# First layer's attention: three engines in program order, the modulation in single steps between key blocks

## The chip, the cores and the metric

The kernel runs on one core of a Trainium2 chip. The metric is device time in microseconds (us), the median of several runs. The engines are TensorE (PE in the profile, its weight loads PEld), VectorE (DVE), ScalarE (ACT), GpSimd (POOL) and SyncE (SP), which issues nearly all DMAs.

## The reference

Two layers; each is attention, then a gated MLP with a causal convolution, with RMSNorms and a modulation by a conditioning vector `c`. The first layer's attention is "stick-breaking" (16 heads of 64, 512 positions, width 1024):

```python
mod = jnp.einsum('bd,dm->bm', silu(c), w_mod[i]) + b_mod[i]
sh_a, sc_a, gt_a, sh_f, sc_f, gt_f = jnp.split(mod, 6, axis=-1)
h = modulate(rmsnorm(x, g_mix_pre[i]), sh_a, sc_a)
q, k, v = (split_heads(t) for t in jnp.split(jnp.einsum('bsd,de->bse', h, w_qkv[i]), 3, axis=-1))
# stick-breaking, for each block of queries:
log_beta = log_sigmoid(z); log_1mb = where(strict, log_sigmoid(-z), 0)
after = cumsum(log_1mb, reverse=True) - log_1mb
a = where(strict, exp(log_beta + after), 0)          # times v
o = merge_heads(a @ v) @ w_o[i]
x = x + gt_a * rmsnorm(o, g_mix_post[i])             # then the MLP, with sh_f, sc_f, gt_f
```

## The kernel before

All matrix products are made of three fp32r matmuls: each operand is split in a high part (a cast on ACT, L192) and a low part (a subtraction, L193), by DVE or, for most weights of the attention, by GpSimd (`wh`, `wl`; for late tiles of `w_o` `sh`, `sl`).

`attention` runs over heads. In the pass for head h, for each of four query blocks `qb` from 3 down to 0 (512, 384, 256, 128 keys wide), `scores` writes a PSUM bank `ps` (L380); `stick` makes two sigmoids on ACT (`bt`, `ps`: L389, L390), a running product on DVE (a scan, L391, into `om` for the two wide blocks, else in place) and a product `bt` (L392; on GpSimd for the two wide blocks, else on DVE). Between the blocks the head before (`late`) goes on: `transposed` turns its probabilities on PE (`pa`, L414) and splits them (`ah` on ACT, `al` on DVE). After the fourth block `weighted` multiplies them with the values into `po` (L429 with `ah`, L430 with `al`); the result goes through ACT and DVE (`of`, L434 and L435), and after an odd head it is split (`oh`, `ol`). Between all of this `fill` puts pieces of other PE work, `UNITS` many a head (some ten): projections of later heads (`proj`, bank `pqk`, 8 pieces each; then `queries` makes `qa`, `qb` or `keys` makes `kh`, `kl`, by turns on ACT and DVE from that one bank), values (`pv`, `v`) and the start of the output projection (`project`).

`mod_part` computes one sixth of the modulation in steps: it sums eight tiles of `w_mod` (512 KB each, DMA into `wm`, three buffers shared with `ah`, `al` and `gp` of this part) times an element of `csil` on DVE (`acc`, 128x1024, L143; the first of some parts L141), splits the sum (L146, L148), sums over partitions with matmuls `pm` (L160, L161), and makes a row (`gt`, L163) or columns (eight diagonals, L128). In the first layer `Background` does three parts (`GT_A`, `SC_F`, `SH_F`) behind the attention's heads: three steps at the end of each pass for a head, from head 2 on, at a lower priority.

`Stream` loads weight tiles (`raw`: DMA into `wf`, three buffers) two tiles ahead of use and splits them at once.

What sets the order: PE and SP run in the order in which the program is written, in the whole kernel. In `begin`, ahead of the first attention, ACT, DVE and GpSimd do as well; elsewhere a scheduler orders these three by priorities (the place in the program) and its own idea of when things are ready.

Of the kernel before, what the change touches and what calls it, by code (L numbers as in the profile page):

```python
# [37 lines left out]
def trunk(ctx, tc, x, c, w_mod, b_mod, g_mix_pre, g_mix_post, w_qkv, w_o, w_fg, b_fg,  # L38
# [8 lines left out]
    def nm(s):  # L47
        serial[0] += 1
        return f"{s}_{serial[0]}"
# [10 lines left out]
    def t4(s, dt=F32):  # L60
        return sb.tile([P, D], dt, tag="t4", name=nm(s), bufs=3)
# [65 lines left out]

        nc.vector.tensor_tensor_reduce(junk(P), src, idn, 1.0, 0.0, op0=ALU.mult, op1=ALU.add, accum_out=dst)  # L128

    def mod_part(l, comp):  # L130
        row = comp in (GT_A, GT_F)
        acc = sb.tile([P, D], F32, tag="acc", name=nm("acc"), bufs=1)
        lo_c = comp * D
        if row:
            nc.gpsimd.memset(acc, 0.0)
            nc.sync.dma_start(acc[0:1, :], b_mod[l : l + 1, lo_c : lo_c + D])
        for d in range(ND):
            w = t4("wm")
            nc.sync.dma_start(w, w_mod[l, d * P : (d + 1) * P, lo_c : lo_c + D])
            if d == 0 and not row:  # L140
                nc.vector.tensor_scalar(acc, w, csil[:, 0:1], None, op0=ALU.mult)  # L141
            else:
                nc.vector.scalar_tensor_tensor(acc, w, csil[:, d : d + 1], acc, op0=ALU.mult, op1=ALU.add)  # L143
            yield
# [27 lines left out]
        made[l, comp] = res  # L172

    class Background:
        def __init__(self, parts):
            self.gens = [mod_part(*p) for p in parts]

        def step(self, n=1):
            while n and self.gens:
# [15 lines left out]
    def raw(src, inner):  # L195
        w = sb.tile([P, 1024], F32, tag="wf", name=nm("wf"), bufs=3)
        v = w.rearrange("p (a b) -> p a b", b=inner)
        nc.sync.dma_start(v, src)
        return w

    def w_tile(src, inner, engine=None):
        w = raw(src, inner)
        hi = sb.tile([P, 1024], F32R, tag="wh", name=nm("wh"), bufs=3)
        lo = sb.tile([P, 1024], F32R, tag="wl", name=nm("wl"), bufs=3)
        split(hi, lo, w, engine)
        return hi, lo

    def w_slots(src, inner, engine=None):
        w = raw(src, inner)
        res = []  # L210
# [4 lines left out]
        return res  # L215

    class Stream:
        def __init__(self):
            self.keys, self.fns, self.got, self.at = [], [], {}, 0

        def add(self, key, fn):
            self.keys.append(key)
            self.fns.append(fn)

        def upto(self, i):
            while self.at <= min(i, len(self.keys) - 1):
                self.got[self.keys[self.at]] = self.fns[self.at]()
                self.at += 1

        def need(self, key, ahead=2):  # L230
            i = self.keys.index(key)
            self.upto(i + ahead)
            return self.got[key]

    ws = Stream()
# [283 lines left out]
    def attention(l, qk, vt, ot, filler, units, bg):  # L519
# [4 lines left out]
        for h in range(NH + 1):  # L524
# [17 lines left out]
            for qb in range(NT - 1, -1, -1):  # L542
                if h < NH:
                    ps, n = scores(l, hd, qb, qk[p, 0], qk[p, 1])
                    probs[qb] = stick(ps, n) if l % 2 == 0 else fox(ps, qb, cums[h])
                    fill()
                if turned:
                    at = next(turned)
                    fill()
            fill(2)  # L550
            if late:
                drain(turned)
# [2 lines left out]
                        fill()  # L555
            fill(12)
            late = (probs, h)
            with tc.high_priority(offset=-100):
                bg.step(3 if h > 1 else 0)


    def begin(vt, qk):
# [196 lines left out]

    cums_of = {}  # L760
    for l in range(DEPTH):
        bg = Background([(l, GT_A), (l, SC_F), (l, SH_F)] if l == 0 else [])
        scale = -0.125 if l % 2 else 0.125
        vt, qk = {}, {}
        if l == 0:
# [172 lines left out]
```

## Time and profile before

| | before |
|---|---|
| median of 3 runs | 1312.1 us (1309.64 to 1312.73) |
| profiled execution | 1313.45 us, span 1311.7 us |
| mean granted clock of TensorE | 0.99 |
| PE, DVE, ACT, POOL busy, share of the span | 95%, 63%, 47%, 22% |
| first layer's attention, first score matmul of head 0 to that of head 14 | 74.17 to 253.62 us |

A row of a timeline has start (us), duration (us), engine, line, operation, output and inputs (buffer numbers left out), shape, count, and in brackets the idle time just before with what ended it. A row of the waits has who waited for whom, us in total, times, and the longest. Durations of neighbours on one engine overlap by some hundredths.

### The profile page before, as it was taken

Reading aid. Unit: us, or ns where it says so; the run is one execution under the profiler, and the core shown is the slowest. Engines: PE = TensorE matmul, PEld = TensorE weight load, DVE = VectorE, ACT = ScalarE, POOL = GpSimd, SP = SyncE. Lnnn points to the kernel's source line nnn. Section 1 sums busy time; section 2 is a strip of 40 time slices with the busy share of each in tenths; the row PEclk is TensorE's granted clock in tenths of the full one; section 3 lists DMA queues with packets and bytes.
Section 4 is the critical chain, followed back from the end, with each engine's and each line's share of the span. In section 5 each row is a group of like instructions: output and inputs, shape, how many; then the busy total and the mean of one; then the engine's idle time right before and its main releaser. Section 6 shows DMA issues by size and latency. Waiting matters only on the chain.

```text
span 1311.7 us, 17096 instructions
## 1 busy us (share of the span) xinstructions
PE 1252.5 (95%) x6244; PEld 1050.0 (80%) x6244; DVE 829.0 (63%) x1455; ACT 617.3 (47%) x1182; POOL 293.7 (22%) x326
## 2 busy tenths in 40 slices
PE   5898978999999999999999999999999999999997
PEld 4676867789887788888888789887898888888886
DVE  7978889756868887532344777786775444443233
ACT  5466645757434333321356556666753333332121
POOL 3586544631000000000022744554100000000000
PEclk8999988999999999999999999999999999999999
DMA  8652533221667766332411533332254333333331
GB/s 273 197 177 97 162 113 128 81 85 45 225 209 245 235 219 217 111 96 97 144 35 43 169 113 104 106 114 80 80 190 131 97 96 96 97 97 97 96 96 64
DMA packets 174857, 169.19 MB, mean 129 GB/s; under 512 B 6937, under 2 KB 151729, under 8 KB 174773
## 3 DMA queue, kind: packets, MB, share of 16 engines
q1 hardware_dynamic: 174596, 168.04, 41.0%
q8 instruction: 49, 0.80, 0.2%
q14 instruction: 36, 0.29, 0.1%
q10 hardware_dynamic: 176, 0.07, 0.0%
HBM read 165.92 MB, written 2.16 MB: 128 GB/s over the span
## 4 chain that ended last, share of the span: by engine, by line
PE 64%; DVE 9%; ACT 5%; DMA 3%; issue 2%; POOL 1%; POOLq 0%; DVEq 0%; SPq 0%; ACTq 0%
PE pgu L267 11%; PE pgu L268 11%; PE pgu L266 11%; PE pd L267 6%; PE pd L268 6%; PE pd L266 6%; PE pqk L266 2%; PE pqk L267 2%; PE pqk L268 1%; PE ps L380 1%; DMA wf<-in_w_ffn_gate_dram 1%; DVE fx L404 1%; PE pa L414 1%; ACT junk L287 1%; PE po L430 1%
## 5 line engine op out<-in xcount | busy, mean ns | idle before, releaser
L192 ACT CAST wh<-wf 128x1024 fp32r<-128x1024 f32 (+2 forms) x178 | 185.3, 1041 | 317.2 <-PE pgu L267 151.1
L193 DVE TENSOR_TENSOR wl<-wf,wh 128x1024 fp32r<-128x1024 f32 x122 | 149.2, 1223 | 217.9 <-ACT wh L192 215.6
L267 PE MATMUL pgu<-htl,wh 128*128 128x512 f32 (+1 forms) x736 | 276.9, 376 | 0.5 <-DVE htl L328 0.5
L266 PE MATMUL pgu<-hth,wh 128*128 128x512 f32 (+1 forms) x736 | 276.9, 376 | 0.0
L268 PE MATMUL pgu<-hth,wl 128*128 128x512 f32 (+1 forms) x736 | 276.9, 376 | 0.0
L193 POOL TENSOR_TENSOR wl<-wf,wh 128x1024 fp32r<-128x1024 f32 (+3 forms) x56 | 132.8, 2376 | 230.4 <-ACT wh L192 218.6
L267 PEld LDWEIGHTS pgu<-htl,wh 128*128 128x128 f32 x736 | 138.9, 189 | 26.1 <-DVE htl L328 0.9
L266 PEld LDWEIGHTS pgu<-hth,wh 128*128 128x128 f32 x736 | 139.0, 189 | 25.0
L268 PEld LDWEIGHTS pgu<-hth,wl 128*128 128x128 f32 x736 | 138.8, 189 | 25.2
L279 POOL TENSOR_TENSOR r<-v,mhalf 128x1 f32<-128x1 f32 x32 | 17.8, 557 | 450.7 <-DVE v L275 450.7
L266 PE MATMUL pd<-wh,yh 128*128 128x512 f32 x288 | 112.0, 389 | 0.0
L267 PE MATMUL pd<-wl,yh 128*128 128x512 f32 x288 | 112.0, 389 | 0.0
L268 PE MATMUL pd<-wh,yl 128*128 128x512 f32 x288 | 112.0, 389 | 0.0
L143 DVE SCALAR_TENSOR_TENSOR acc<-wm,csil,acc 128x1024 f32<-128x1024 f32 x74 | 101.1, 1366 | 15.2 <-DMA wm<-in_w_mod_dram 14.6
L266 PE MATMUL pqk<-hth,wh 128*128 128x512 f32 (+1 forms) x240 | 100.9, 420 | 0.0
L268 PE MATMUL pqk<-hth,wl 128*128 128x512 f32 (+1 forms) x240 | 93.9, 391 | 0.5 <-POOL wl L193 0.5
L267 PE MATMUL pqk<-htl,wh 128*128 128x512 f32 (+1 forms) x240 | 93.6, 390 | 0.0
L850 ACT ACTIVATE cv<-cv 128x512 f32<-128x512 f32 x44 | 27.8, 632 | 102.7 <-DVE cv L849 98.0
L266 PE MATMUL pv<-wh,hth 128*128 128x256 f32 (+1 forms) x224 | 69.9, 312 | 0.1
L268 PE MATMUL pv<-wh,htl 128*128 128x256 f32 (+1 forms) x224 | 67.1, 299 | 1.1 <-DVE htl L664 1.0
L267 PE MATMUL pv<-wl,hth 128*128 128x256 f32 (+1 forms) x224 | 66.9, 299 | 0.0
L851 DVE TENSOR_TENSOR cv<-cv,pgu 128x512 f32<-128x512 f32 x44 | 30.2, 686 | 52.9 <-PE pgu L268 46.9
(194 smaller groups left out, 2513.4 us busy)
## 6 DMA issues: line engine op xcount, KB each, us to landing
wm<-in_w_mod_dram SPq DMA_DIRECT2D x80, 512.0 KB, 4.9
wf<-in_w_ffn_gate_dram SPq DMA_DIRECT2D x44, 512.0 KB, 4.4
wf<-in_w_ffn_up_dram SPq DMA_DIRECT2D x44, 512.0 KB, 3.7
wf<-in_w_ffn_down_dram SPq DMA_DIRECT2D x44, 512.0 KB, 3.5
wf<-in_w_qkv_dram SPq DMA_DIRECT2D x41, 512.0 KB, 3.8
wm<-in_w_mod_dram SPq DMA_DIRECT2D x32, 256.0 KB, 4.2
wf<-in_w_o_dram SPq DMA_DIRECT2D x16, 512.0 KB, 3.6
cum<-cumd SPq DMA_DIRECT2D x16, 512.0 KB, 4.1
```

The costliest lines, as they stand in the source:

```text
L143: nc.vector.scalar_tensor_tensor(acc, w, csil[:, d : d + 1], acc, op0=ALU.mult, op1=ALU.add)
L192: nc.scalar.copy(hi, src)
L193: (engine or nc.vector).tensor_tensor(lo, src, hi.bitcast(F32), op=ALU.subtract)
L266: nc.tensor.matmul(ps, ah, bh, start=first, stop=False)
L267: nc.tensor.matmul(ps, ah, bl, start=False, stop=False)
L268: nc.tensor.matmul(ps, al, bh, start=False, stop=last)
L279: nc.gpsimd.tensor_tensor(r, v, mhalf, op=ALU.pow)
L287: nc.scalar.activation(junk(), src, AF.Square, scale=1.0 / 32.0, accum_out=m)
L380: nc.tensor.matmul(ps[:, :n], q[hd][:, qs], k[hd][i][:, :n], start=i == 0, stop=i == 1)
L404: nc.vector.tensor_scalar(t[:, :n], t[:, :n], r, None, op0=ALU.mult)
L850: nc.scalar.activation(a, a, AF.Silu)
L851: nc.vector.tensor_tensor(a, a, u, op=ALU.mult)
```

## The change

In the first layer's attention ACT, DVE and GpSimd now also run in program order. The modulation takes one step behind each of the query blocks 3, 2 and 1 of the heads from 2 on, not three at the end of a pass; each `wm` load is written one step ahead of its use, and a part has twelve steps (the first only loads). A weight tile's DMA is still written two tiles ahead, but its split now comes with the next tile's load (`lag`). Elsewhere `lag` and `ahead` are 0.

```diff
-    def mod_part(l, comp):
+    def mod_part(l, comp, ahead=0):
...
+        tiles = []
+
+        def load(d):
+            tiles.append(t4("wm"))
+            nc.sync.dma_start(tiles[d], w_mod[l, d * P : (d + 1) * P, lo_c : lo_c + D])
+
+        load(0)
+        if ahead:
+            yield
         for d in range(ND):
-            w = t4("wm")
-            nc.sync.dma_start(w, w_mod[l, d * P : (d + 1) * P, lo_c : lo_c + D])
+            if d + ahead < ND and d + ahead:
+                load(d + ahead)
+            w = tiles[d]
...
     def w_tile(src, inner, engine=None):
         w = raw(src, inner)
+        yield
...
         def upto(self, i):
-            while self.at <= min(i, len(self.keys) - 1):
-                self.got[self.keys[self.at]] = self.fns[self.at]()
+            while len(self.loaded) <= min(i, len(self.keys) - 1):
+                self.loaded.append(self.fns[len(self.loaded)]())
+                next(self.loaded[-1])
+                self.parts(len(self.loaded) - 1 - self.lag)
+
+        def parts(self, i):
+            while self.at <= i:
+                self.got[self.keys[self.at]] = next(self.loaded[self.at])
                 self.at += 1
 
         def need(self, key, ahead=2):
             i = self.keys.index(key)
             self.upto(i + ahead)
+            self.parts(i)
             return self.got[key]
...
                 if turned:
                     at = next(turned)
                     fill()
+                if qb and h > 1:
+                    bg.step()
...
             late = (probs, h)
-            with tc.high_priority(offset=-100):
-                bg.step(3 if h > 1 else 0)
...
-        bg = Background([(l, GT_A), (l, SC_F), (l, SH_F)] if l == 0 else [])
+        bg = Background([(l, GT_A), (l, SC_F), (l, SH_F)] if l == 0 else [], 1)
...
-        attention(l, qk, vt, ot, filler, UNITS[l], bg)
+        if l == 0:
+            ws.lag = 1
+            with tc.manual_schedule(engines={mybir.EngineType.Activation, mybir.EngineType.DVE, mybir.EngineType.Pool}):
+                attention(l, qk, vt, ot, filler, UNITS[l], bg)
+            ws.lag = 0
+        else:
+            attention(l, qk, vt, ot, filler, UNITS[l], bg)
```

Line numbers rise by up to 28. Three places show what moves; the numbers behind names count tiles and differ between the kernels.

DVE in head 3, from the 384-wide `al` to the head's end, before: the last `al` (128 wide, 1225 from 1278) stands fourth from the scans' end.

```order
L193 TENSOR_TENSOR al_1225<-pa_1220,ah_1224 128x384
L193 TENSOR_TENSOR al_1225<-pa_1278,ah_1224 128x128
L359 SCALAR_TENSOR_TENSOR qa_1228<-pqk_1137,qa_1228 64x512
L359 SCALAR_TENSOR_TENSOR qb_1229<-pqk_1137,qb_1229 64x512
L193 TENSOR_TENSOR al_1260<-pa_1256,ah_1259 128x256
L391 SCALAR_TENSOR_TENSOR ps_1244<-ps_1244,zid 128x256
L392 TENSOR_TENSOR bt_1247<-bt_1247,ps_1244 128x255
L391 SCALAR_TENSOR_TENSOR ps_1266<-ps_1266,zid 128x128
L392 TENSOR_TENSOR bt_1269<-bt_1269,ps_1266 128x127
```

And the same place now:

```order
L203 TENSOR_TENSOR al_1225<-pa_1220,ah_1224 128x384
L381 SCALAR_TENSOR_TENSOR qa_1228<-pqk_1146,qa_1228 64x512
L381 SCALAR_TENSOR_TENSOR qb_1229<-pqk_1146,qb_1229 64x512
L153 SCALAR_TENSOR_TENSOR acc_1063<-wm_1204,csil,acc_1063 128x1024
L413 SCALAR_TENSOR_TENSOR ps_1247<-ps_1247,zid 128x256
L414 TENSOR_TENSOR bt_1250<-bt_1250,ps_1247 128x255
L203 TENSOR_TENSOR al_1263<-pa_1259,ah_1262 128x256
L153 SCALAR_TENSOR_TENSOR acc_1063<-wm_1244,csil,acc_1063 128x1024
L413 SCALAR_TENSOR_TENSOR ps_1272<-ps_1272,zid 128x128
L414 TENSOR_TENSOR bt_1275<-bt_1275,ps_1272 128x127
L203 TENSOR_TENSOR al_1225<-pa_1284,ah_1224 128x128
```

The last `al`, for which PE's `po` waits, moved from ahead of both narrow scans to behind them, and an accumulation stands in each gap.

DVE from the end of head 6 into head 7, before:

```order
L193 TENSOR_TENSOR al_1674<-pa_1724,ah_1673 128x128
L143 SCALAR_TENSOR_TENSOR acc_1611<-wm_1772,csil,acc_1611 128x1024
L193 TENSOR_TENSOR v_1751<-pv_1717,v_1751 128x4x64
L143 SCALAR_TENSOR_TENSOR acc_1611<-wm_1775,csil,acc_1611 128x1024
L435 TENSOR_TENSOR of_1316<-po_1746,of_1316 64x512
L143 SCALAR_TENSOR_TENSOR acc_1611<-wm_1913,csil,acc_1611 128x1024
L193 TENSOR_TENSOR ol_1315<-of_1316,oh_1314 128x512
L143 SCALAR_TENSOR_TENSOR acc_1611<-wm_1916,csil,acc_1611 128x1024
L391 SCALAR_TENSOR_TENSOR om_1782<-ps_1778,zid 128x512
L143 SCALAR_TENSOR_TENSOR acc_1611<-wm_1919,csil,acc_1611 128x1024
L193 TENSOR_TENSOR al_1800<-pa_1794,ah_1799 128x512
```

And now:

```order
L203 TENSOR_TENSOR al_1671<-pa_1727,ah_1670 128x128
L203 TENSOR_TENSOR v_1754<-pv_1720,v_1754 128x4x64
L457 TENSOR_TENSOR of_1313<-po_1749,of_1313 64x512
L203 TENSOR_TENSOR ol_1312<-of_1313,oh_1311 128x512
L413 SCALAR_TENSOR_TENSOR om_1776<-ps_1772,zid 128x512
L203 TENSOR_TENSOR al_1794<-pa_1788,ah_1793 128x512
L153 SCALAR_TENSOR_TENSOR acc_1647<-wm_1705,csil,acc_1647 128x1024
```

Four accumulations that stood ahead of head 7's first scan are gone from there; they come one by one behind the `al` of the blocks.

ACT from the end of head 4 into head 5, before:

```order
L192 CAST wh_1434<-wf_1432 128x1024
L358 ACTIVATE qa_1426<-pqk_1345 64x512
L358 ACTIVATE qb_1427<-pqk_1345 64x512
L434 COPY of_1039<-po_1442 64x512
L192 CAST oh_1037<-of_1039 128x512
L389 ACTIVATE bt_1474<-ps_1471 128x511
L390 ACTIVATE ps_1471<-ps_1471 128x512
```

And now:

```order
L380 ACTIVATE qa_1430<-pqk_1342 64x512
L380 ACTIVATE qb_1431<-pqk_1342 64x512
L202 CAST wh_1438<-wf_1336 128x1024
L456 COPY of_1037<-po_1446 64x512
L202 CAST oh_1035<-of_1037 128x512
L411 ACTIVATE bt_1465<-ps_1462 128x511
L412 ACTIVATE ps_1462<-ps_1462 128x512
```

The weight's cast moved from ahead of `qa` to between `qb` and `of`.

More of the change, by code (lines that the diff above doesn't have):

```diff
@@ L174, in trunk, with __init__ @@
     class Background:
-        def __init__(self, parts):
-            self.gens = [mod_part(*p) for p in parts]
+        def __init__(self, parts, ahead=0):
+            self.gens = [mod_part(*p, ahead) for p in parts]
         def step(self, n=1):
@@ L205, in w_tile @@
         split(hi, lo, w, engine)
-        return hi, lo
+        yield hi, lo
     def w_slots(src, inner, engine=None):
         w = raw(src, inner)
+        yield
         res = []
@@ L214, in w_slots @@
             res.append((hi, lo))
-        return res
+        yield res
     class Stream:
         def __init__(self):
-            self.keys, self.fns, self.got, self.at = [], [], {}, 0
+            self.keys, self.fns, self.got, self.at, self.lag, self.loaded = [], [], {}, 0, 0, []
         def add(self, key, fn):
```

## The prediction, made before the changed kernel ran

> **What bounds the kernel now.** I read the page first, then busy time head by head, then the waits of TensorE, then the timelines of VectorE (DVE) and ScalarE (ACT) where it waits.
>
> ```profile
> span 1311.7 us, 17096 instructions
> PE 1252.5 (95%) x6244; PEld 1050.0 (80%) x6244; DVE 829.0 (63%) x1455; ACT 617.3 (47%) x1182; POOL 293.7 (22%) x326
> ```
>
> TensorE (PE) is busy 95% of the span, so over the whole program it sets the end. The first layer's attention is the exception. The windows below begin where the first score matmul of head 1, 2, 3, 4, 5, 7 and 9 starts; the sum runs over heads 1 to 13. Columns: length, busy time (count) of PE, PEld, DVE, ACT, POOL, granted clock, DMA share, GB/s.
>
> ```profile
> 83.67:96.30 12.63, 11.21 (x57) 8.87 (x56) 12.14 (x20) 7.88 (x17) 12.16 (x15) 1.00 0.71 249
> 96.30:110.03 13.73, 10.99 (x56) 8.54 (x57) 13.44 (x20) 7.85 (x17) 9.78 (x14) 1.00 0.48 161
> 110.03:123.23 13.20, 11.88 (x62) 9.33 (x61) 11.55 (x15) 8.79 (x18) 5.41 (x6) 1.00 0.34 112
> 123.23:133.89 10.66, 10.66 (x58) 8.90 (x58) 9.11 (x18) 8.04 (x19) 8.16 (x12) 1.00 0.01 2
> 133.89:144.87 10.98, 10.98 (x69) 9.63 (x68) 8.46 (x16) 8.67 (x19) 6.25 (x10) 1.00 0.00 0
> ...
> 155.62:174.30 18.68, 13.86 (x70) 11.54 (x70) 16.65 (x20) 8.24 (x18) 8.11 (x9) 0.82 0.66 219
> ...
> 186.42:204.94 18.52, 12.66 (x60) 9.77 (x59) 16.38 (x27) 8.01 (x19) 8.80 (x12) 0.94 0.37 105
> ...
> sum 169.95, PE 150.16 PEld 126.55 DVE 149.46 ACT 104.16 POOL 94.51; mean PE 11.55 PEld 9.73 DVE 11.50 ACT 8.01 POOL 7.27
> ```
>
> Heads 4 and 5 carry no accumulation of the modulation: PE never stops, 10.7 to 11 us each. Heads 1 to 3 carry about three steps each and take 12.6 to 13.7 us, with DVE nearly full. Heads 7 and 9 got four or five steps and take 18.6. PE idles 169.95 - 150.16 = 19.8 us, and what it waits for is DVE:
>
> ```profile
> PE ps L380 <- DVE om L391: 7.8, 4, 4.8
> PE po L430 <- DVE al L193: 4.0, 5, 2.5
> DVE acc L143 <- DMA wm<-in_w_mod_dram: 2.3, 4, 1.2
> ```
>
> So DVE is a second bound here, 149.5 us of 170. The question is how much of it each order leaves idle.
>
> **The change, part by part.** One head in the new order is a ring. DVE does scan, `al`, step three times, a fourth scan, its product, and the last `al`; PE's last `po` matmul needs that `al`; the next head's scores stand behind that matmul in PE's fixed order; ACT makes the sigmoids of those scores; DVE's first scan waits for them. I price the ring from DVE's rows in head 2, the nearest row that there is:
>
> ```profile
> 99.83 1.21 DVE L391 TENSOR_TENSOR_SCAN om<-ps,zid 128x512 f32<-128x512 f32 x1
> 100.95 0.66 DVE L193 TENSOR_TENSOR al<-pa,ah 128x512 fp32r<-128x512 f32 x1
> 101.54 1.75 DVE L143 SCALAR_TENSOR_TENSOR acc<-wm,csil,acc 128x1024 f32<-128x1024 f32 x1
> 103.21 0.95 DVE L391 TENSOR_TENSOR_SCAN om<-ps,zid 128x384 f32<-128x384 f32 x1
> 104.07 0.37 DVE L120 COPY colB<-pcol 128x88 f32<-128x88 f32 x2
> 104.37 0.54 DVE L193 TENSOR_TENSOR al<-pa,ah 128x384 fp32r<-128x384 f32 x1
> 104.83 1.77 DVE L143 SCALAR_TENSOR_TENSOR acc<-wm,csil,acc 128x1024 f32<-128x1024 f32 x1
> 106.53 0.68 DVE L391 TENSOR_TENSOR_SCAN ps<-ps,zid 128x256 f32<-128x256 f32 x1
> 107.13 0.66 DVE L371 TENSOR_TENSOR kl<-pqk,kh 64x512 fp32r<-64x512 f32 x1
> 107.72 0.40 DVE L392 TENSOR_TENSOR bt<-bt,ps 128x255 f32<-128x255 f32 x1
> 108.04 0.27 DVE L193 TENSOR_TENSOR al<-pa,ah 128x128 fp32r<-128x128 f32 x1
> 108.44 0.69 DVE L371 TENSOR_TENSOR kl<-pqk,kh 64x512 fp32r<-64x512 f32 x1
> 109.16 0.42 DVE L193 TENSOR_TENSOR al<-pa,ah 128x256 fp32r<-128x256 f32 x1
> 109.50 0.42 DVE L391 TENSOR_TENSOR_SCAN ps<-ps,zid 128x128 f32<-128x128 f32 x1
> 109.96 0.29 DVE L392 TENSOR_TENSOR bt<-bt,ps 128x127 f32<-128x127 f32 x1
> 110.37 1.28 DVE L143 SCALAR_TENSOR_TENSOR acc<-wm,csil,acc 128x1024 f32<-128x1024 f32 x1
> ```
>
> From the first scan to the last `al` 9.7 us pass. Two accumulations take 1.67 and 1.70 of them from start to start, `kl` 0.59 and 0.72, the copies 0.30; 4.7 are left. Here the last scan and product (0.9 from start to start, some 0.6 of it work) come behind both late `al`; in the new order they come ahead of the last one. So the stretch without modulation is 5.3 us.
>
> An accumulation counts 1.68, not the 1.2 that it takes undisturbed (1.28 in the last row above, less the 0.08 by which rows overlap), because the new order puts it right where it stood here: behind an `al` that follows a scan, while GpSimd runs that scan's product. How hard the two engines block each other:
>
> ```profile
> 187.20 3.19 DVE L143 SCALAR_TENSOR_TENSOR acc<-wm,csil,acc 128x1024 f32<-128x1024 f32 x1 [0.35 <-DMA wm<-in_w_mod_dram]
> ...
> 186.95 2.36 POOL L193 TENSOR_TENSOR wl<-wf,wh 128x1024 fp32r<-128x1024 f32 x1
> ```
>
> This one started just behind a `wl`, stood until that ended at 189.31 and then ran its 1.1 us. The third step of a head, behind the 256-wide product that DVE does itself, meets no product of GpSimd but may meet such a `wl`, since GpSimd too now goes in program order; I price it the same. The Trainium skill, page "SBUF — State Buffer", section "Who interferes with whom", states this as a rule: a DVE instruction with two SBUF inputs and a GpSimd one that reads SBUF exclude each other for a whole instruction. The trace agrees (3.19 us beside a 2.36 us `wl`). By the rule a collision with a `wl` costs up to the 2.4 us of it, and the sum would be some 4 us higher than with my 0.48.
>
> Each head also ends one projection on average (two instructions that ACT and DVE do in turn on one PSUM bank). In program order nothing fills DVE's gap between them:
>
> ```profile
> 121.63 0.69 DVE L359 SCALAR_TENSOR_TENSOR qb<-pqk,qb 64x512 fp32r<-64x512 f32 x1 [0.66 <-ACT qb L358]
> ```
>
> That is 0.68 + 0.66 + 0.69 = 2.0 us, in the stretch or at the head's turn. The turn itself, after an even and after an odd head's output (`oh` makes ACT wait for DVE once more):
>
> ```profile
> 96.14 0.33 PE L430 MATMUL po<-al,v 128*128 128x128 f32 x1 [0.40 <-DVE al L193]
> ...
> 123.86 0.58 ACT L434 COPY of<-po 64x512 f32<-64x512 f32 x1
> ...
> 125.71 1.22 DVE L391 TENSOR_TENSOR_SCAN om<-ps,zid 128x512 f32<-128x512 f32 x1 [0.43 <-ACT ps L390]
> ...
> 262.38 0.58 ACT L434 COPY of<-po 64x512 f32<-64x512 f32 x1 [0.93 <-PE po L430]
> ...
> 265.48 1.22 DVE L391 TENSOR_TENSOR_SCAN om<-ps,zid 128x512 f32<-128x512 f32 x1 [0.42 <-ACT ps L390]
> ```
>
> From `of` to the scan 1.85 and 3.10 us; with the last `po` and its two handovers (0.45) in front 2.3 and 3.55, 2.9 on average. Before, the scheduler put accumulations into this gap (one stands at 110.37, ahead of head 3's scan) and took the late `al` ahead of the late scans. The new order does neither: a step stands only between key blocks, where DVE is already late.
>
> The other steps, and the cast that leads each weight's split (line, engine, tile, shape, count, busy us, mean ns):
>
> ```profile
> L148 DVE TENSOR_TENSOR al<-acc,ah 128x1024 fp32r<-128x1024 f32 x3 | 4.6, 1518 | 1.4 <-ACT ah L146 1.4
> L128 DVE CUSTOM_DVE_ANT_0 junk<-pm,zid 128x128 bf16<-128x128 f32 x16 | 4.6, 286 | 1.2 <-PE pm L161 1.0
> ...
> L192 ACT CAST wh<-wf 128x1024 fp32r<-128x1024 f32 (+2 forms) x178 | 185.3, 1041 | 317.2 <-PE pgu L267 151.1
> ```
>
> *A head with three accumulations* (heads 3, 4, 7, 8, 11, 12): 5.3 + 3 x 1.68 + 2.0 + 2.9 + 0.2 for handing over = 15.4. *A head with the narrowing and eight diagonals* (9, 13): 1.5 and 8 x 0.33 (0.29 and the read behind it) instead of 5.0 gives 14.5. *Light heads* (2, 5, 6, 10; of the twelve steps of a part one only loads, and some are short): I take 2.8, between one and two accumulations, which gives 13.2. Without any step the same sum gives 10.4, below PE's 10.7, which fits heads 4 and 5. So heads 1 to 13 take 10.7 + 6 x 15.4 + 2 x 14.5 + 4 x 13.2 = 184.9 against 169.95, 15 us more.
>
> The rest I price at nothing. *Loads a step ahead:* `wm` has three buffers, so its DMA already starts three steps early; at most the 2.3 us that DVE waited for `wm` come back, hidden behind the ring. On SP's queue the `wm` and `wf` loads change places by one or two entries; the buffers, not the queue, release them, and the cover is gone only if a `wf` stands behind a blocked `wm` for a whole head. *Splitting a weight one tile later (lag):* PE needs it a projection later, eight of the some ten pieces of filler in a head's 10.7 us; cast and `wl` take 1.04 + 2.36. *The sums' matmuls (`pm`) inside heads 5, 9, 13:* PE waits there for DVE's narrowing, ahead of scores that DVE would not reach earlier. *The clearing of `acc` on GpSimd in head 2* is seen at worst by the one product behind it. *The three extra steps* lengthen the modulation by one head; its last result is needed only after the attention.
>
> The profiled execution took 1313.45 us (span 1311.7), 1.35 above the median of the runs. 1313.45 + 14.9 - 1.35 = 1327.
>
> **The rivals.** *Faster, one head like heads 1 to 3 of before.* If program order leaves DVE as little idle as there (0.8 us a head) and spreads what heads 7 and 9 had in a lump, heavy heads take 13.2 and light ones 12.0: 10.7 + 8 x 13.2 + 4 x 12.0 = 164.3, 5.7 us less, 1306. For it speaks that 18.6 us twice is clearly bad and cannot come back; against it that those heads had a step in the turn. It decides at (169.95 - 10.7) / 12 = 13.3 us a head. *Faster, PE alone:* all waits go, 19.8 us, 1292; DVE's 149.5 us plus the ring's turns speak against it. *Same:* accumulations and GpSimd don't collide systematically; 24 steps x 0.48 = 11.5 less, 1315.5, and with a turn that ACT shortens, 1312. *Slower still:* a heavy head stops PE for 4 to 5 us at one place, and the granted clock fell to 0.82 in the head with the 4.8 us wait; if the `po` and the scores that close the ring then run at half speed, they take their 0.33 and 0.2 us once more, some 0.5 us a head, 1333.
>
> The Trainium skill, page "TensorE: Matmul & The Clock Gate", section "What's actually happening", has the clock at half rate after an idle window of about 3.4 us; the 0.82 of head 7 agrees, and by the rule eight heads would be hit.
>
> **How the numbers follow.** My ring: 0.50 at 1327, and 0.14 with the clock's part, 1333. Same: 0.14. Like heads 1 to 3: 0.17. PE alone: 0.05. A run of this kernel tells about 0.3% from no change; so slower 0.64, same 0.14, faster 0.22. The range 1304 to 1341 leaves out the last case, part of the one before it, and the upper end of the ring, where each `wl` hits a step. The ring's own range is 1318 to 1341.
>
> **What would show it.** Right: heads 3, 4, 7 and 8 near 15 us, PE's waits for `al` (L430 before) several times their 4.0 us and the largest of its waits, accumulations at 1.6 us or more on average, DVE idle for ACT's `ps` and `of` at each head's turn. Wrong: heads 2 to 13 even and below 13.3 us. My weakest term is the turn: if ACT reaches the next scores sooner than in these rows, each head gives up to 1 us back, and twelve heads bring the time to the edge of no change.

## The result, and the profile after

The changed kernel takes 1362.5 us (median; 1361.4 to 1367.3) against 1312.4 of the kernel before (1309.6 to 1312.7) beside it: a ratio of 1.0393, 95% interval 1.0374 to 1.0412. It is slower, as forecast, but by 50 us where the forecast had 15, and outside the range (1304 to 1341).

The page of the profiled execution (1362.56 us; columns as before):

```profile
span 1360.8 us, 17052 instructions
...
PE 1267.9 (93%) x6244; PEld 1060.2 (78%) x6244; DVE 831.6 (61%) x1455; ACT 620.9 (46%) x1182; POOL 287.0 (21%) x326
```

The same instructions as before keep PE busy 15 us longer (1252.5 before): part of them ran at a lower clock. The rest of the loss is idle time. Busy time by head, from the first score matmul of heads 1, 2, 3, 4, 5, 7 and 10 on; the sum runs over heads 1 to 13:

```profile
83.71:94.43 10.72, 10.72 (x57) 8.85 (x56) 8.29 (x17) 6.62 (x15) 7.52 (x14) 1.00 0.00 0
94.43:113.38 18.95, 11.85 (x58) 9.11 (x57) 11.08 (x19) 8.72 (x18) 9.61 (x13) 0.87 0.53 169
113.38:129.37 15.99, 13.97 (x60) 11.53 (x61) 12.94 (x17) 8.10 (x17) 6.31 (x9) 0.83 0.43 131
129.37:146.47 17.10, 11.71 (x57) 9.01 (x58) 13.66 (x17) 7.78 (x17) 6.69 (x10) 0.99 0.22 63
146.47:168.27 21.80, 15.72 (x68) 12.67 (x68) 12.50 (x19) 10.65 (x20) 9.14 (x13) 0.81 0.37 119
...
179.87:201.50 21.63, 14.38 (x71) 11.94 (x70) 11.49 (x16) 8.13 (x17) 7.69 (x8) 0.76 0.54 175
...
233.10:255.36 22.26, 14.13 (x73) 12.53 (x73) 11.56 (x19) 9.09 (x19) 9.54 (x13) 0.77 0.22 66
...
sum 221.05, PE 167.76 PEld 138.77 DVE 152.14 ACT 109.08 POOL 90.78; mean PE 12.90 PEld 10.67 DVE 11.70 ACT 8.39 POOL 6.98
```

Heads 1 to 13 take 221.05 us against 169.95: 51 us, the whole difference. PE is idle for 221.05 - 167.76 = 53.3 us of them (19.8 before, 33.5 more) and busy 17.6 us longer. All head lengths:

| head | 1 | 2 | 3 | 4 | 5 | 6 | 7 | 8 | 9 | 10 | 11 | 12 | 13 | sum |
|---|---|---|---|---|---|---|---|---|---|---|---|---|---|---|
| before | 12.6 | 13.7 | 13.2 | 10.7 | 11.0 | 10.8 | 18.7 | 12.1 | 18.5 | 12.7 | 14.2 | 10.1 | 11.7 | 170.0 |
| forecast | 10.7 | 13.2 | 15.4 | 15.4 | 13.2 | 13.2 | 15.4 | 15.4 | 14.5 | 13.2 | 15.4 | 15.4 | 14.5 | 184.9 |
| after | 10.7 | 19.0 | 16.0 | 17.1 | 21.8 | 11.6 | 21.6 | 16.0 | 15.6 | 22.3 | 15.9 | 12.1 | 21.5 | 221.1 |
| after, no lag, clearing early | 12.4 | 13.6 | 15.9 | 15.1 | 16.0 | 10.8 | 14.1 | 16.2 | 15.6 | 14.6 | 14.6 | 12.9 | 17.2 | 189.0 |

Heads 3, 8, 9 and 11 are within 1.1 us of the forecast. Heads 2, 5, 7, 10 and 13 are 6 to 9 us above it; heads 6 and 12 are 1.6 and 3.3 below. What PE waits for between 70 and 330 us (waiter, releaser: total, times, longest):

```profile
PE po L452 <- DVE al L203: 16.1, 13, 2.0
PE pv L288 <- ACT wh L202: 7.2, 2, 6.2
PE pqk L290 <- POOL wl L203: 6.3, 2, 4.8
PE po L451 <- ACT ah L202: 5.2, 1, 5.2
PE pm L171 <- DVE al L158: 4.8, 3, 1.6
PE pv L289 <- POOL bt L410: 4.0, 2, 2.1
PE pm L170 <- ACT ah L156: 2.4, 3, 1.4
PE pqk L288 <- ACT wh L202: 2.4, 1, 2.4
```

The largest is the wait for `al` that the forecast named (4.0 us before). The waits for `wh` and `wl`, halves of weight tiles, did not exist before; they add up to 15.9 us in these rows. (The 4.0 us put down to a `bt` are also a `wl`: the next rows show one.) One of them, in head 10, in the timelines of ACT, DVE, POOL and PE:

```profile
239.65 0.58 ACT L391 CAST kh<-pqk 64x512 fp32r<-64x512 f32 x1
245.15 0.58 ACT L391 CAST kh<-pqk 64x512 fp32r<-64x512 f32 x1 [4.91 <-DVE kl L393]
245.75 1.04 ACT L202 CAST wh<-wf 128x1024 fp32r<-128x1024 f32 x1
...
242.59 1.27 DVE L153 SCALAR_TENSOR_TENSOR acc<-wm,csil,acc 128x1024 f32<-128x1024 f32 x1
...
244.44 0.67 DVE L393 TENSOR_TENSOR kl<-pqk,kh 64x512 fp32r<-64x512 f32 x1
...
246.93 2.34 POOL L203 TENSOR_TENSOR wl<-wf,wh 128x1024 fp32r<-128x1024 f32 x1 [0.51 <-POOL kh L392]
...
246.85 0.58 PE L288 MATMUL pv<-wh,hth 128*128 128x256 f32 x1 [6.24 <-ACT wh L202]
249.33 0.58 PE L289 MATMUL pv<-wl,hth 128*128 128x256 f32 x1 [1.90 <-POOL bt L410]
```

ACT's second `kh` waits for DVE's `kl`. DVE reaches `kl` at 244.44, since in its program order two accumulations, two narrow scans with their products and two `al` stand ahead. Behind `kh` on ACT stands the cast of a weight; behind the cast stands the subtraction on GpSimd; PE waits for both, 8.1 us together. The cast itself waited for no DMA: it ran as soon as ACT came to it.

Head 2 has another cause. From SP's queue, POOL and DVE:

```profile
101.34 0.25 SPq L136 DMA_DIRECT2D acc<-in_b_mod_dram  x1
101.68 1.29 SPq L141 DMA_DIRECT2D wm<-in_w_mod_dram  x3
...
100.36 0.95 POOL L135 MEMSET acc<- 128x1024 f32 x1
...
105.85 1.28 DVE L153 SCALAR_TENSOR_TENSOR acc<-wm,csil,acc 128x1024 f32<-128x1024 f32 x1 [4.71 <-DMA wm<-in_w_mod_dram]
```

GpSimd clears `acc` at 100.36, behind head 2's first product; the load of `b_mod`'s row into `acc` waits for that on SP, the three `wm` loads wait behind it in SP's queue, and DVE stands 4.71 us for the first of them.

Last, the clock. The windows around the stall in head 10:

```profile
243.00:245.00 2.00, 0.00 (x0) 0.00 (x0) 1.97 (x4) 0.00 (x0) 0.00 (x0) 1.00 0.66 215
245.00:247.00 2.00, 0.15 (x1) 0.15 (x1) 0.81 (x2) 1.80 (x3) 0.68 (x2) 0.52 0.75 240
...
254.00:255.00 1.00, 1.00 (x6) 1.00 (x6) 0.00 (x0) 0.00 (x0) 0.00 (x0) 0.50 0.00 0
256.00:257.00 1.00, 1.00 (x12) 1.00 (x10) 0.69 (x1) 0.24 (x2) 0.00 (x0) 1.00 0.00 0
```

PE stands from 240.6; the granted clock is 0.5 by 247 and stays there until after 255. The price shows in matmuls of one shape: those of `pv` (128x256) start every 0.12 us ahead of the stall and every 0.21 us at 250. An estimate of what this costs in heads 1 to 13, PE's busy time times what the granted clock lacks of 1, summed over quarters of a microsecond: 21.0 us, and 5.5 in the kernel before. So most of the 17.6 us is the clock.

### The profile page after: what moved, and what is told of

The parts are those of the page before. It is cut to its first block, busy times and chain, and to the rows that moved or that the text cites. A ratio compares the mean times of both kernels' runs of the same rounds, so it can differ in the third digit from the quotient of the medians.

```text
span 1360.8 us, 17052 instructions
## 1 busy us (share of the span) xinstructions
PE 1267.9 (93%) x6244; PEld 1060.2 (78%) x6244; DVE 831.6 (61%) x1455; ACT 620.9 (46%) x1182; POOL 287.0 (21%) x326
## 4 chain that ended last, share of the span: by engine, by line
PE 66%; DVE 15%; ACT 7%; DMA 4%; issue 4%; POOL 2%; SPq 1%; POOLq 0%; DVEq 0%; ACTq 0%
PE pgu L289 10%; PE pgu L290 10%; PE pgu L288 10%; PE pd L289 5%; PE pd L290 5%; PE pd L288 5%; DMA wm<-in_w_mod_dram 2%; DVE acc L153 2%; PE pqk L290 2%; PE pqk L288 2%; DVE om L413 2%; PE pqk L289 2%; PE ps L402 2%; ACT wh L202 2%; PE po L289 1%
## 5 line engine op out<-in xcount | busy, mean ns | idle before, releaser
L202 ACT CAST wh<-wf 128x1024 fp32r<-128x1024 f32 (+2 forms) x178 | 184.9, 1041 | 295.7 <-PE pd L290 134.7
L153 DVE SCALAR_TENSOR_TENSOR acc<-wm,csil,acc 128x1024 f32<-128x1024 f32 x74 | 101.5, 1372 | 19.9 <-DMA wm<-in_w_mod_dram 19.4
L203 DVE TENSOR_TENSOR al<-pa,ah 128x512 fp32r<-128x512 f32 (+3 forms) x128 | 60.9, 479 | 5.2 <-ACT ah L202 4.6
```

Of the source, the lines that this page charges most:

```text
L202: nc.scalar.copy(hi, src)
L203: (engine or nc.vector).tensor_tensor(lo, src, hi.bitcast(F32), op=ALU.subtract)
```

## The experiments

"Beside before" is the ratio to the kernel before, run beside it, with its 95% interval. Runs were made in groups. The kernel before differs by some 2 us from group to group (1311.8 to 1314.1), so between groups the ratios are the better measure.

### Two parts undone, in program order

Without the lag (the changed kernel, one line):

```diff
-            ws.lag = 1
+            ws.lag = 0
```

> The changed kernel with the lag alone undone: a weight tile is again split as soon as its DMA is written, still in program order. Late-split theory: heads 5, 7, 10 and 13 lie 30.9 us above my ring's price, heads 6 and 12 5.0 below it; without the lag these 26 us go, 1362 becomes about 1336 (1332 to 1342), and PE's waits for wh and wl (18 us together in the stretch 70 to 330) fall below 3. Rival, the order itself: the splits wait for the engine's program order in any case, and the time moves from one wait to another; 1355 or more, with wh and wl still PE's largest waits or `al` above 25.

With the modulation's first step ahead of the attention:

```diff
         if l == 0:
+            bg.step()
             ws.lag = 1
...
-                if qb and h > 1:
+                if qb and h > 1 and (h, qb) != (2, 3):
                     bg.step()
```

> The changed kernel with the first step of the modulation (clearing of acc on GpSimd, the load of b_mod's row and of the first wm) written ahead of the attention, and nothing else. Queue theory: in head 2 the row's load stood on SP behind GpSimd's clearing, and the wm loads behind it; head 2 falls from 18.95 to 13 to 14, 5 to 6 us in all, 1357. Rival, the ring: head 2 is a heavy head like the others and its wait turns into another; 16 us or more there, 1360 to 1362.

Both edits:

> The changed kernel with both undone: no lag, and the first step ahead of the attention. If the excess over my forecast is those two and nothing more, 1327 to 1334, with heads 3, 4, 8, 9, 11 still at 15 to 17 us and PE's waits for `al` at some 16 us. If the two overlap (a head that waits for a weight would otherwise wait for the ring), 1340 to 1350.

| | us | beside before |
|---|---|---|
| no lag | 1335.5 | 1.0154 (1.0127 to 1.0181) |
| first step ahead | 1357.2 | 1.0328 (1.0306 to 1.0350) |
| both | 1329.8 | 1.0120 (1.0099 to 1.0141) |

Against the changed kernel's 1362.5 the lag costs 27.0 us, the clearing 5.2, both 32.7. The changed kernel ran in another group; by the ratios the three are 31, 9 and 36. Within the one group of these three kernels the lag costs 27.5 (1357.2 to 1329.8) and the clearing 5.7 (1335.5 to 1329.8). So they add, and each came out near what the heads above the forecast had said. Without the lag no wait for a `wh` of a weight is left and of `wl` one of 1.1 us. With both undone head 2 takes 13.6 us, and the waits of PE and the sum over heads 1 to 13 are

```profile
PE po L452 <- DVE al L203: 18.0, 13, 2.4
PE pm L171 <- DVE al L158: 4.8, 3, 1.6
PE po L451 <- ACT ah L202: 3.7, 2, 3.3
PE pm L170 <- ACT ah L156: 3.5, 2, 2.2
```

```profile
sum 188.95, PE 157.48 PEld 132.50 DVE 151.18 ACT 108.93 POOL 92.39; mean PE 12.11 PEld 10.19 DVE 11.63 ACT 8.38 POOL 7.11
```

This is the kernel that the forecast had priced: 184.9 in the heads and 1327. Head by head the two differ by up to 2.8 us, in both directions. The remaining runs ask whether it is slow for the reason given.

### The ring: what in program order makes a head long

All of these have no lag and the first step ahead. Steps out of the heads:

```diff
-                if qb and h > 1 and (h, qb) != (2, 3):
+                if qb and h > NH:
                     bg.step()
```

> Program order, no lag, and no step of the modulation inside the heads (all but the first run after the attention, so only the heads' lengths say something, not the time). If the steps stretch a ring that otherwise hides behind PE (my price without steps was 10.4 us, below PE's 10.7): heads 2 to 13 at 10.6 to 11.5 us, 140 us in all for heads 1 to 13 and PE hardly waiting for `al`. If program order alone costs, by the late `al` and the turn: 12 to 13 us a head, 155 or more.

Its heads 2 to 13 take 9.1 to 12.4 us:

```profile
sum 146.09, PE 141.48 PEld 121.35 DVE 104.36 ACT 101.69 POOL 83.53; mean PE 10.88 PEld 9.33 DVE 8.03 ACT 7.82 POOL 6.43
```

This is one execution (1344.5 us, with the steps behind the attention), and near the first expectation: PE waits only 1.4 us for `al`, but heads 1 to 13 take 6 us more than the 140 expected. So program order by itself is cheap, as long as DVE has 8 us of work a head. The steps bring 151.2 - 104.4 = 46.8 us of DVE work into these heads and lengthen them by 188.95 - 146.09 = 42.9, as if nearly all of the added work lay on the path. It is not a proof: with the steps PE is busy 16.0 us longer too, by their `pm` and a lower clock.

The third step of a head at the end of the pass:

```diff
-                if qb and h > 1 and (h, qb) != (2, 3):
+                if qb > 1 and h > 1 and (h, qb) != (2, 3):
                     bg.step()
...
             late = (probs, h)
+            bg.step(h > 1)
```

> No lag, first step ahead of the attention, and the third step of a head moved from behind the 256-wide block to the end of the pass, in program order: it then stands between the `of` of DVE and the next head's first scan. My ring: DVE idles there some 2.9 us less its own work, an accumulation of 1.2 us fits, and a heavy head gets 1.2 to 1.7 shorter; about 1313 to 1318 against 1329.8. If the turn has no room (the scan comes later by the step): 1327 to 1331.

1329.4 (1.0138; 1.0113 to 1.0163): no gain, the second expectation. Heads 2, 3, 4, 7, 8 and 10 to 13 do become shorter, by 0.3 to 2.3 us and 8.0 together, but heads 5 and 9, where a part's `pm` falls, become longer by 3.7 and 2.8.

The fourth block's late work ahead of its scores:

```diff
+                if turned and l == 0 and not qb:
+                    at = next(turned)
+                    fill()
                 if h < NH:
...
-                if turned:
+                if turned and (l or qb):
                     at = next(turned)
                     fill()
```

> No lag, first step ahead of the attention, and for the fourth block the head before goes on first: its last transposition, `ah` and `al` stand ahead of the fourth block's scores, sigmoids, scan and product. My ring: the last `al` comes 0.9 us earlier (scan and product move into the turn, where DVE idles), and `po` and the next scores with it; 12 heads, about 11 us less, 1317 to 1321. If DVE's sum sets the head's length and not the chain to the last `al`: 1327 to 1331, PE's waits for `al` smaller but another wait in their place.

1328.1 (1.0125; 1.0107 to 1.0144). Heads 2, 3, 4, 7, 8, 12 and 13 are shorter by 0.6 to 0.8 each, close to the 0.9 of the forecast's ring, and head 10 by 3.5; heads 5, 9 and 11 lose 3.1, 0.6 and 3.5. PE's clock is 0.73 in head 5, and 0.89 without the edit. Of the 11 us expected, 1.6 came by the times (1329.8 to 1328.1) and nothing by the ratios (1.0120 and 1.0125): the second expectation.

Two empty steps between a part's narrowing and `pm`:

```diff
         yield
+        for _ in range(2 * ahead):
+            yield
         for h in range(2):
```

> No lag, first step ahead of the attention, program order, and two empty steps between the narrowing of a part's sum (ah, al) and the matmuls pm that read it. In the kernel without them PE waits for pm's operands 8.3 us in heads 5, 9 and 13, then runs at half clock. If those waits cost what they are: heads 5, 9 and 13 fall from 16 to 17 to 13 to 14.5 us, 7 to 9 us in all and up to 5 more by the clock, 1316 to 1323. If my step was right (PE waits there ahead of scores that DVE would not reach earlier): the wait moves to the last `al`, 1327 to 1331.

1326.9 (1.0111; 1.0090 to 1.0131). The waits for `pm` are gone, but PE's waits for `al` rise from 18.0 to 24.0. Heads 1 to 13 take 180.6 us, 8.3 less; of this, heads 5, 9 and 13 give 3.3, 0.5 and 1.7. But the modulation is now six steps longer, so that 6.9 us of DVE's work (151.2 to 144.3) have left these heads, and head 14 takes 13.5 us instead of 8.8. Net 2.9 us, or 1.2 by the ratios: as the second expectation had it, the wait moved to the last `al`.

All of these edits together:

> Program order with everything of the runs so far that shortened a head: no lag, first step ahead, third step at the end of the pass, the head before going on ahead of the fourth block, and two empty steps ahead of pm. If the terms add (ring 0.65 to 1 a head from each of the two orders, pm's waits and the half clock behind them gone): 12.2 to 13 us a head, 160 to 165 in heads 1 to 13, 1301 to 1308. If DVE's program order keeps the ring in any arrangement: 1318 or more.

1322.0 (1.0069; 1.0044 to 1.0095), the second expectation; 174.7 us in heads 1 to 13, and a long head 14 once more (14.8). No arrangement of program order that was tried is as fast as the kernel before.

### Which engine's order

The kernel before with program order alone (three steps at the end of a pass):

```diff
-        attention(l, qk, vt, ot, filler, UNITS[l], bg)
+        if l == 0:
+            with tc.manual_schedule(engines={mybir.EngineType.Activation, mybir.EngineType.DVE, mybir.EngineType.Pool}):
+                attention(l, qk, vt, ot, filler, UNITS[l], bg)
+        else:
+            attention(l, qk, vt, ot, filler, UNITS[l], bg)
```

> The kernel before with one part of the change alone: ACT, DVE and GpSimd in program order in the first layer's attention; the three steps stay at the end of a pass, no lag, no load ahead. My ring with three accumulations in the turn instead of the stretch: 5.3 + 2.0 + about 5.2 + 0.2 = 12.7 for a heavy head, 12 for a light one; heads 1 to 13 some 160 to 166 us and 1302 to 1309. If three steps in a row only push the next head's first scan back by their whole length, 14 us and 1314 or more.

1340.0 (1.0216; 1.0198 to 1.0234), the second expectation, and 26 us above its 1314. Heads 3, 5, 8 and 12 take 18 to 24 us. PE's waits for `pm`'s `ah` are 11.6 us, the longest 7.2, and for scans (`om`) 19.7, as they would be if three steps in a row push back all that is behind them. Steps between the blocks and loads a step ahead are thus together better in program order (1335.5 without the lag, 1.0154); they are not what costs.

With no lag and the first step ahead, and fewer engines named in `manual_schedule(engines={...})`:

> No lag, first step ahead, and program order for DVE alone; the scheduler orders ACT and GpSimd. If the ring is DVE's (its late `al` and its turn): 1325 to 1331, as with all three. If ACT's order (standing at kh and qb behind DVE's kl and qa) or GpSimd's makes the ring: 1308 to 1316.

> The complement: program order for ACT and GpSimd, DVE by the scheduler, no lag, first step ahead. If the ring is DVE's: 1306 to 1314, near the scheduler's order of all three. If it is ACT's or GpSimd's: 1322 or more, with PE's waits for `ah` or ACT's for `kl` and `qa` the largest.

> No lag, first step ahead, program order for ACT alone; the scheduler orders DVE and GpSimd. With ACT and GpSimd in program order it was 1325, with none (and the lag) 1309. If ACT's order is what costs there (ACT stands at kh and qb behind DVE's kl and qa, 20 and 12 us): 1321 to 1327. If it is GpSimd's (products and weight splits in order): 1306 to 1313.

> The scheduler's order of all three engines, no lag, first step ahead of the attention; steps between the blocks and loads a step ahead stay. Against the same kernel with the lag (1309) it tells what the lag costs when nothing stands in program order: if late splits hurt only because they queue behind waiting work, 1306 to 1312, no difference; if they hurt by themselves, 1300 to 1304. Against the same kernel in program order (1329.8) it gives the price of program order with all else equal: my ring, 15 us, or more.

| program order for | us | beside before |
|---|---|---|
| ACT, DVE, GpSimd | 1329.8 | 1.0120 (1.0099 to 1.0141) |
| DVE | 1334.0 | 1.0164 (1.0142 to 1.0185) |
| ACT, GpSimd | 1325.4 | 1.0097 (1.0074 to 1.0121) |
| ACT | 1323.0 | 1.0064 (1.0051 to 1.0077) |
| none | 1315.8 | 1.0015 (1.0001 to 1.0030) |

Of 1312 us, DVE's order costs 20 (1.0164 - 1.0015), ACT's 6, ACT's and GpSimd's together 11, and all three 14: they don't add. GpSimd's order alone was not run. The base in the last line is 8 us above the scheduler's best (1307.3 us, below), through heads 0 and 1, which DVE's program order leaves undisturbed; against that best DVE's order costs 28. In heads 2 to 13 alone, DVE's order adds 28 us to the kernel with none, ACT's 11, ACT's and GpSimd's 10, all three 22.

The first expectation asked whether the ring is DVE's. PE's waits for `al`, which close the ring, say yes; between 70 and 300 us, with DVE's order, with ACT's and GpSimd's, and with none:

```profile
PE po L452 <- DVE al L203: 24.3, 15, 2.8
```

```profile
PE po L452 <- DVE al L203: 2.4, 4, 1.1
```

```profile
PE po L452 <- DVE al L203: 3.3, 5, 2.0
```

But ACT's order costs by itself, as the second and third runs came out on its side, and the ring had no term for that. With ACT's order alone PE waits 11.6 us for `pm`'s operands (6.8 for `ah`, 4.8 for `al`), where with none only 1.3 us were ahead of `pm`. The fourth run (1315.8) met neither expectation, because of heads 0 and 1. ACT's own waits for DVE grow with program order; heads 0 to 13, first with all three in program order, then with none:

```profile
ACT qb L380 <- DVE qa L381: 21.0, 7, 6.0
ACT kh L391 <- DVE kl L393: 19.5, 8, 6.1
```

```profile
ACT kh L391 <- DVE kl L393: 13.8, 7, 3.7
...
ACT qb L380 <- DVE qa L381: 8.2, 7, 1.8
```

### The scheduler's order with the steps between the blocks

The changed kernel without `manual_schedule`:

```diff
-            with tc.manual_schedule(engines={mybir.EngineType.Activation, mybir.EngineType.DVE, mybir.EngineType.Pool}):
-                attention(l, qk, vt, ot, filler, UNITS[l], bg)
+            attention(l, qk, vt, ot, filler, UNITS[l], bg)
```

> The changed kernel with the scheduler's order of ACT, DVE and GpSimd in place of program order; steps between the blocks, loads a step ahead and the lag stay. If program order is the cause (late splits and the clearing are late only because they stand in order behind waiting work): 1305 to 1318, near before. If the placement of the steps or the lag is the cause by itself: 1335 or more, with PE waiting for wh and wl or for `al` as in the changed kernel.

The same without the lag:

> The scheduler's order, steps between the blocks, loads ahead, no lag, and the first step where the change has it (head 2). Without the first step ahead, heads 0 to 3 should again be like those with the lag (9.5, 13.5, 13.3, 12.1): if the first step ahead is what lengthened head 1 to 19.4 us in the scheduler's order, 1306 to 1311, as with the lag; if it is the missing lag that did it, 1313 to 1317.

A fourth buffer for `wm`, `ah`, `al`, `gp` (with the lag, the first step in head 2):

```diff
-NS = 44
+NS = 42
...
-        return sb.tile([P, D], dt, tag="t4", name=nm(s), bufs=3)
+        return sb.tile([P, D], dt, tag="t4", name=nm(s), bufs=4)
```

> The scheduler's order, steps between the blocks, loads ahead, lag, first step in head 2, and the fourth buffer for the modulation's tiles. If the first step ahead lengthened heads 0 to 2 by some 7 us, and the fourth buffer shortens heads 4 to 13 by 1 to 2: 1306 to 1309, the fastest so far. If the fourth buffer's accumulations, now in heads 4 to 6 too, cost there what head 7 gains: 1309 to 1312.

and with the first step ahead, without and with the fourth block's late work first:

> The scheduler's order with steps between the blocks, loads ahead, lag, first step ahead of the attention, and a fourth buffer for the tiles of the modulation (wm, ah, al, gp; two slots of 44 fewer make the room). Head 7 takes 20.6 us with three buffers because ah and al hold two of them until pm, so that the next sum's loads come in a lump. If that is so: heads 7 and 9 fall from 20.6 and 16.4 to 12 to 14 us, the others rise by about 1, 1299 to 1304. If DVE's sum bounds the stretch in any case: 1307 to 1310.

> As the one with the fourth buffer, and for the fourth block the head before goes on first, so that the last `al` is written ahead of the last scan. In program order that shortened a head by 0.65 us. If it does in the scheduler's order too: 3 to 7 us below the one without. If the scheduler takes that `al` early in any case: within 2 us of it.

| scheduler's order, steps between blocks | us | beside before |
|---|---|---|
| lag, first step in head 2 | 1309.0 | 0.9958 (0.9939 to 0.9977) |
| no lag, first step in head 2 | 1307.3 | 0.9952 (0.9936 to 0.9968) |
| no lag, first step ahead | 1315.8 | 1.0015 (1.0001 to 1.0030) |
| fourth buffer, lag, first step in head 2 | 1307.0 | 0.9954 (0.9937 to 0.9971) |
| fourth buffer, lag, first step ahead | 1315.0 | 1.0008 (0.9996 to 1.0020) |
| and the late work first | 1318.8 | 1.0031 (1.0019 to 1.0043) |

The first two came out as expected (1309.0 near before; 1307.3, so that the first step ahead is what lengthened head 1), and the fourth buffer with the first step in head 2 too (1307.0), though no faster than the others by its ratio. With the first step ahead as well, 1315.0 and 1318.8 missed both of their expectations.

Three things follow. The steps between the blocks and the loads ahead, together with the steps' priority, which is no longer lowered, are a gain of 0.4 to 0.5% when the scheduler orders the engines; none of the three was run alone. These are the fastest kernels here. The lag costs nothing there (1309.0 and 1307.3, by their ratios the same): it costs 27 us only with program order. The first step ahead, which saves 5 us in program order, costs 8 in the scheduler's, since accumulations then come into heads 0 and 1 (head 1 takes 19.4 us instead of 13.4).

The lumps of accumulations in heads 7 and 9 stay without the fourth buffer; heads 1 to 13 with three buffers and the lag (the row of head 7, the sum), then heads 4, 7 and 8 with four:

```profile
155.51:176.13 20.62, 14.11 (x69) 11.82 (x70) 17.21 (x20) 9.25 (x19) 7.70 (x9) 0.83 0.41 137
...
sum 166.34, PE 149.54 PEld 126.38 DVE 146.08 ACT 105.48 POOL 94.07; mean PE 11.50 PEld 9.72 DVE 11.24 ACT 8.11 POOL 7.24
```

```profile
122.51:138.07 15.56, 12.38 (x58) 10.02 (x58) 12.21 (x16) 8.27 (x18) 9.60 (x13) 0.89 0.27 92
...
162.94:174.88 11.94, 11.76 (x70) 9.94 (x70) 10.18 (x18) 8.41 (x20) 6.83 (x9) 1.00 0.18 52
174.88:192.28 17.40, 13.05 (x55) 10.07 (x55) 12.64 (x18) 8.86 (x19) 6.44 (x10) 0.80 0.73 236
```

Head 7 falls to 11.9 as expected, but heads 4 and 8 rise from 10.6 and 10.9 to 15.6 and 17.4, and the total is the same. That the number of buffers decides where the lumps fall is shown; that a smoother spread is worth something is not.

## Why the prediction was wrong in size

*The lag, priced at nothing: the step that failed, 27 us.* It said that PE needs a tile "a projection later, eight of the some ten pieces". That holds for the first tile of a row of projections. But `values` takes two tiles in its first four pieces, and the projection behind it takes the next; with the lag the second tile of the values is first split when `values` begins, and the next projection's tile when that projection begins. So the split stands at the moment of need. The waits are at these places: at `pv` in heads 5 and 10, at the next projection (`pqk`) in head 7, and in head 13 at the output projection, which takes a new tile every two pieces (0.9 us for `wh`, 2.0 for `wl`). The other half of the step, "cast and `wl` take 1.04 + 2.36", took the cast's duration where its place in ACT's order counts: behind `kh`, which stood 4.9 us for DVE. The same lag under the scheduler's order, where the cast need not stand behind `kh`, cost nothing.

*The clearing of `acc`, priced at nothing: 5 us.* "Seen at worst by the one product behind it" looked at GpSimd's queue only. The load into `acc` waits for the clearing at the head of SP's queue, and all `wm` and `wf` loads stand behind it. The forecast named that danger for `wf` behind a blocked `wm`, not for `wm` behind the row of `b_mod`.

*The ring: its sum was right, its mechanism half.* With those two undone the time is 1329.8 and heads 1 to 13 take 189.0; the forecast's ring had 1327 and 184.9. Part of this is luck: heads 1, 5 and 13 lie 1.7 to 2.8 us above the forecast and heads 6, 7 and 12 lie 1.3 to 2.5 below, and 7.3 us are longer busy time of PE, for which the ring had no term. For the ring speak PE's waits for `al`, which go with DVE's order (24.3 with it alone, 2.4 without), the gain of 0.6 to 0.8 per head from the earlier `al`, the steps' 42.9 us for 46.8 us of DVE's work, and DVE's waits for ACT's `of` and `ps` at the head's turn, which rise from 9.7 and 3.7 us to 20.9 and 8.7. The forecast's weakest term, the turn, did not hold as told: a step moved there shortened nine heads by 8.0 us together, below the 1.2 to 1.7 each that the turn's 2.9 promised, and two other heads gave 6.5 of it back. And the projection's pair, 2.0 us from DVE's rows, has another side that the forecast left out: ACT stands up to 6.1 us between its two instructions, 40.5 us in all (24.4 before), with `ah` and casts behind it. What that costs no run isolates; DVE's order alone, with ACT's by the scheduler, is no faster (1334.0).

*An accumulation at 1.68:* the size is about right, its reason not. The forecast expected more collisions with GpSimd in the new order, and 1.6 us or more on average. The 128x1024 accumulations between 83 and 305 us, by shape (count, busy us, mean ns, idle ahead), took

```profile
L153 DVE SCALAR_TENSOR_TENSOR acc<-wm,csil,acc 128x1024 f32<-128x1024 f32 x22 | 34.9, 1588 | 4.7 <-DMA wm<-in_w_mod_dram 4.7
```

```profile
L143 DVE SCALAR_TENSOR_TENSOR acc<-wm,csil,acc 128x1024 f32<-128x1024 f32 x22 | 34.5, 1566 | 2.5 <-DMA wm<-in_w_mod_dram 2.3
```

1.59 us on average now (the first row) and 1.57 before. Collisions come in both orders and are no part of the difference.

*`pm` in heads 5, 9, 13, priced at nothing:* right within 1 to 3 us. The waits are real (8.3 us without the lag and with the early clearing), but when `pm` is moved away 6.0 us of them come back as waits for `al`, as the forecast's reason had it.

*The clock, a rival at 0.5 us a head:* too small for long stalls. PE was busy 17.6 us longer in heads 1 to 13, a third of the loss (7.3 without the lag and with the early clearing).

*Loads a step ahead, three steps more:* right. Without the blocked load DVE's wait for `wm` at the accumulations is 0.0 instead of 2.3, and head 14 takes 8.8 us against 8.6.

*The rival "faster"* did not happen with program order. With the scheduler's order 1307 to 1309 lie near its 1306, but not by the even spread of which it spoke: head 7 rises from 18.7 to 20.6, and heads 8 to 12 fall from 67.7 to 60.9 us. Why they do is not shown.

Open remain: why DVE's order alone costs more than all three orders together (its waits for `al` are 24.3 us against 18.0); why the fourth buffer moves the long heads to 4 and 8. The clock's part was read from the windows and not isolated by a run.

## What to carry to other kernels

Before fixing an order by hand, ask of every instruction that moves what stands behind it on its own queue, and for how long the instruction ahead of it can wait: a 1 us cast "needed later" cost 8 us of PE time because it stood behind a cast that waited for another engine. When a prefetch is made lazier, look for the consumer that takes two items at once, since that one sets the lead. And try the parts of a change apart: here the steps between the blocks with their early loads were worth 0.5% under the scheduler, and the order around them cost 28 us (1335.5 against 1307.3), with the lag 53 (1362.5 against 1309.0).

## What the runs showed of the hardware

After a stall of PE the granted clock stays at 0.5 for longer than the stall: it is 0.5 for some 8 us behind the 6.24 us stall in head 10 (with one of 1.9 us in it), and for some 6 us behind a stall of 3.33 us in the kernel without the lag and with the early clearing.

The length of a stall alone does not decide. In that kernel one wait of 2.35 us was enough, and so were two of 1.95 and 1.61 us within 5 us; two of 1.62 and 1.61 us within 4 us were not, and in the kernel before one of 2.68 us was not. What decides is how the idle time falls on a grid. Every stretch at 0.5 in heads 1 to 13 of the kernel before, the changed one and the one with both undone lasted 3.4, 6.8 or 10.2 us, and within a run all begin and end on one grid of 3.41 us. Windows of that grid in the kernel with both undone: the one with the waits of 1.95 and 1.61 us and the one behind it, then the two with those of 1.62 and 1.61:

```profile
137.73:141.14 3.41, 0.79 (x4) 0.65 (x5) 3.31 (x8) 0.00 (x0) 0.35 (x3) 1.00 0.10 13
141.14:144.55 3.41, 3.41 (x11) 2.73 (x11) 1.70 (x3) 2.25 (x4) 1.32 (x1) 0.50 0.98 276
...
250.37:253.78 3.41, 1.79 (x10) 1.29 (x8) 3.38 (x6) 0.45 (x1) 0.59 (x3) 1.00 0.16 65
253.78:257.19 3.41, 1.80 (x12) 1.44 (x10) 2.69 (x6) 0.99 (x2) 0.00 (x0) 1.00 0.00 0
```

In the first window PE is idle for 2.6 us, and the next runs at 0.50; the other two waits fall into two windows with 1.6 us of idle time each, and the clock stays at 1.00. In ten of these traces, between 76 and 270 us, a window with 1.9 us or more of idle time was always followed by half clock and one with 1.3 or less never; in between both occurred. The clock came back after a window with 0.4 us of idle time or less.

The Trainium skill, page "TensorE: Matmul & The Clock Gate", section "What's actually happening", gives a window of about 3.4 us, free-running, both for the fall and for the way back. The grid and the way back agree with it. For the fall it asks for an idle window; here 1.9 us of idle time in a window was enough, and the measurement decides. It calls the ramp's penalty under 1% of a typical span; here PE's longer busy time is 1.3% (17.6 of 1361 us), with a clock below 0.95 in nine of the thirteen heads.
